# Making Strassen's weight sums in DRAM with accumulating transfers, during an earlier phase of the kernel

## The chip, the cores and the metric

The kernel runs on one core of one Trainium2 chip. The metric is the device time of one execution in microseconds (us). The kernel before was timed three times: 2057.39, 2060.06 and 2066.34 us, so its median is 2060.06 us. The profile is of one further execution.

## The reference

Two layers of a diffusion backbone run over 256 latent and 256 context tokens, model width 2048, all float32. Layer 0 is a bidirectional retention layer, layer 1 a windowed attention layer:

```python
for i in range(DEPTH):                      # DEPTH = 2
    mod_l = c_act @ ada_w[i] + ada_b[i]     # shift, scale, gate (latent); mod_c likewise for the context
    h_l = _rms_norm(x, norm_gain[i]) * (1 + sc_l) + sh_l          # h_c likewise
    if i % 2 == 0:
        y_l, y_c = _retention_mixer(h_l, h_c, ret_w_in, ..., ret_w_out, ...)
    else:
        y_l, y_c = _attention_mixer(...)
    x = x + gt_l * y_l
    if i < DEPTH - 1:
        ctx = ctx + gt_c * y_c

def finish(o, g):                           # the end of the retention layer
    on = o * rsqrt(mean(o * o) + EPS) * norm_gain
    return (on * silu(g)) @ w_out           # (512 x 4096) @ (4096 x 2048)
```

The change concerns the last line, the retention layer's output projection, and what runs before it.

## The kernel before, in words

**Precision.** TensorE multiplies in a rounded float32 format. Each operand is split into a high part (rounded, a cast on ACT) and a low part (source minus high, a subtraction on DVE), and products are summed from high x high, high x low and low x high. For a weight tile of 128 x 1024 elements, `split_w` does this: the cast `wh` (L131) and the subtraction `wl` (L112, which is the line of every such subtraction). A weight tile arrives by `load_raw` (L122) on SP's DMA queue into `wraw`; there are three buffers each of `wraw`, `wh` and `wl`.

**Phases, in order of time.** First the modulation of layer 0 and the first projections (to about 133 us); then the eight retention heads (to about 1222 us); then the output projection of the retention layer (to 1630 us); then the attention layer (to 2059 us).

**The heads.** Per head there are a gate, a query-key and a value projection, each of 8 weight pieces (`gemm_ws` or `gemm_ts`). After each piece a `hook` is called; the hooks are numbered by `state["n"]`, and a head has 24 (the first two and the last 16). A hook runs one entry of a list of small tasks: `output_tasks` of the head before (POOL adds up squares at L789 and takes the power `rs` at L239, TensorE then transposes `rs`), `score_tasks` with `decays` (POOL's power `dd`, L736). From the 33rd hook on it also runs two `ada_jobs`: a load `abraw` on SP (L672) and one or two products with running sums on DVE (L675). The program's planner fixes the order in which each engine issues its instructions, by priorities and by its own costs; `tc.issue_after(x)` ties an instruction behind x on x's engine.

**The output projection by Strassen.** The 4096 x 2048 weight is cut into 2 x 2 blocks and the operand likewise (the halves of the contraction, and latent against context tokens). Seven products, M1 to M7, replace eight. `parts` forms the operand sums of each head and puts them into DRAM (`uB_d`); `prep` (L649) loads them and splits them into high and low. Products were done in four stages: (M4, M1), (M5, M7), (M2, M6) and (M3). In `stage`, an output quarter r (0 to 3) takes four contraction quarters kq; for each r, kq and product, `weights` yields a split weight tile and `piece` does 8 high matmuls (L927, 512 columns) and 8 low ones (L924, 256 columns). Weights are loaded by `quarter` (L906, 512 KB each). Where a product needs the sum of two weight blocks, both are loaded and `comb` adds them on POOL (L911). Raw weight tiles go round a `ring` of seven buffers. `done` functions take the accumulators out (`merged` L932 to L937, `added` L941) into `x1`; `residual` (L960) applies the gate and adds the input, `square` (L950, L951) sums squares for the next norm; in the last stage `hook4` modulates the latent tokens for layer 1 (ACT at L1079, POOL through `comb`, then `modulate`).

Of the kernel before, what the change touches and what calls it, by code (L numbers as in the profile page):

```python
# [10 lines left out]
F32 = mybir.dt.float32  # L11
F32R = mybir.dt.float32r
# [9 lines left out]
T = 512  # L22
L = 256
# [28 lines left out]
def backbone(ctx: ExitStack, tc, xT_d, w0_d, wo0_d, w1_d, wo1_d, adaS_d, adaB_d,  # L52
# [39 lines left out]
    gam16 = const.tile([P, 8, 8], F32, name="gam16")  # L92
    lg2 = const.tile([P, 16], F32, name="lg2")

    ng = vec[:, V_NG:V_NG + 32].rearrange("p (l k) -> p l k", l=2)
# [15 lines left out]
    def sub(out, a, hi):  # L111
        return nc.vector.tensor_tensor(out=out, in0=a, in1=hi.bitcast(F32), op=ALU.subtract)  # L112
# [4 lines left out]

    last_lo, last_hi = [None], [None]

# [8 lines left out]
    def split_w(raw):  # L128
        wh = strm.tile([P, 2, 512], F32R, name="wh", tag="wh", bufs=3)
        wl = strm.tile([P, 2, 512], F32R, name="wl", tag="wl", bufs=3)  # L130
        last_hi[0] = nc.scalar.copy(wh, raw).ins  # L131
        last_lo[0] = sub(wl, raw, wh).ins
        return wh, wl

# [473 lines left out]
    def slot_l(s):  # L608
# [7 lines left out]
    R_, T_, h_, H_ = ([(n, i) for i in range(k)] for n, k in (("R", 10), ("T", 5), ("h", 8), ("H", 8)))  # L616
    home = {M4: R_[0:8], M1: R_[8:10] + T_[0:5] + H_[7:8], M5: h_, M7: H_[5:7] + R_[2:8],
            M2: R_[0:2] + R_[8:10] + T_[0:4], M6: T_[4:5] + H_[7:8] + R_[2:8], M3: h_}
    units = {}
# [34 lines left out]
    if True:  # L654
# [32 lines left out]

        jobs = ada_jobs()
        state = {"n": 0}

        def hook():
            state["n"] += 1
            if state["n"] > 32:
# [152 lines left out]
        for h in range(H):  # L846
# [20 lines left out]
            if h == 1:  # L867
                close_top()
        for _ in jobs:
            pass  # L870

# [25 lines left out]
    with tc.tile_pool(name="pc", bufs=1, side="right") as pc:  # L897
# [5 lines left out]

        def quarter(nh, kh, r, kq):
            t = raw_tile()
            nc.sync.dma_start(out=t.rearrange("p a t -> p (a t)"),  # L906
                              in_=wo0_d[nh, kh, r, kq].rearrange("p k c -> p (k c)"))
            return t

        def comb(out, a, b, op):  # L910
            nc.gpsimd.tensor_tensor(out=out, in0=a, in1=b, op=op)  # L911
            return out

# [24 lines left out]

        def added(out, acc):
            for c in (lat, cx):  # L940
                nc.vector.tensor_tensor(out=out, in0=acc[:, c], in1=out, op=ALU.add)  # L941

        def square(kb, c):
# [8 lines left out]

        def residual(kbs):

            xr = raw_tile()
            nc.sync.dma_start(out=xr, in_=xT_d[:, kbs[0]:kbs[-1] + 1, :])
            for i, kb in enumerate(kbs):
                for s in range(2):
                    c = (lat, cx)[s]
                    nc.vector.scalar_tensor_tensor(out=x1[:, kb, c], in0=x1[:, kb, c], scalar=gt0[:, kb, s:s + 1],  # L960
                                                   in1=xr[:, i, c], op0=ALU.mult, op1=ALU.add)
                nc.scalar.dma_start(out=x1_d[kb], in_=x1[:, kb, lat])
                square(kb, lat)

        def stage(ms, weights, done, hook):
            for r in range(4):
                accs = {m: [acc_tile() for _ in range(2)] for m in ms}
                n1, n2 = slice(2 * r, 2 * r + 2), slice(8 + 2 * r, 10 + 2 * r)
                for kq in range(4):
# [4 lines left out]
                    hook(r, kq)  # L974

        def weights1(r, kq):
            b, a = quarter(1, 1, r, kq), quarter(0, 0, r, kq)
            yield split_w(b)
            yield split_w(comb(a, a, b, ALU.add))

        def done1(r, m, accs, n1, n2):
            for j in range(2):
                merged(x1[:, 8 + 2 * r + j, lat if m == M4 else cx], accs[j], neg=(m == M4))
            if m == M1:
                comb(x1[:, n1, lat], x1[:, n2, cx], x1[:, n2, lat], ALU.add)

        def hook1(r, kq):
            if kq == 1:
                prep(M5, [2 * r, 2 * r + 1])
            if (r, kq) == (2, 2):  # L990
                prep(M7, [0, 1])
            if r == 3 and kq > 1:
                prep(M7, [2 * kq - 2, 2 * kq - 1])
# [6 lines left out]
        def done2(r, m, accs, n1, n2):  # L1000
            if m == M5:
                for j in range(2):
                    merged(x1[:, 2 * r + j, cx], accs[j])
            else:
                for j in range(2):
                    added(x1[:, 2 * r + j, lat], accs[j])
                comb(x1[:, n1, lat], x1[:, n1, lat], x1[:, n1, cx], ALU.subtract)

        def hook2(r, kq):
            if r and kq == 2:  # L1010
                residual([2 * r - 2, 2 * r - 1])
            if kq == 1:
                prep(M2, [2 * r, 2 * r + 1])
            if (r, kq) == (2, 2):
                prep(M6, [0, 1])
            if (r, kq) == (0, 0):
                prep(M7, [6, 7])
            if r == 3 and kq > 1:
                prep(M6, [2 * kq - 2, 2 * kq - 1])

        def weights3(r, kq):
            a, b, c = quarter(1, 0, r, kq), quarter(1, 1, r, kq), quarter(0, 0, r, kq)
            yield split_w(comb(b, a, b, ALU.add))
            yield split_w(comb(c, a, c, ALU.subtract))

        def done3(r, m, accs, n1, n2):
            if m == M2:
                t = tmp[:, r % 2]
                for j in range(2):
                    merged(t[:, j], accs[j])  # L1030
                comb(x1[:, n2, lat], x1[:, n2, lat], t, ALU.add)
                nc.vector.tensor_tensor(out=x1[:, n2, cx], in0=x1[:, n2, cx], in1=t, op=ALU.subtract)
            else:
                for j in range(2):
                    added(x1[:, 8 + 2 * r + j, cx], accs[j])

        def hook3(r, kq):
            if (r, kq) == (0, 0):
                prep(M6, [6, 7])
            if kq == 2:  # L1040
                residual([2 * r + 6, 2 * r + 7])
            if kq == 1:
                prep(M3, [2 * r, 2 * r + 1])
# [9 lines left out]

        def weights4(r, kq):
            yield split_w(quarter(0, 0, r, kq))

        def done4(r, m, accs, n1, n2):
            t = tmp4[:, r % 2]
            for j in range(2):
                merged(t[:, j], accs[j])  # L1060
                for kb in (2 * r + j, 8 + 2 * r + j):
                    nc.vector.scalar_tensor_tensor(out=x1[:, kb, cx], in0=t[:, j], scalar=gt0[:, kb, 1:2],
                                                   in1=x1[:, kb, cx], op0=ALU.mult, op1=ALU.add)
                    square(kb, cx)

# [3 lines left out]

        def hook4(r, kq):  # L1070

            if r == 0:
                return
            n = 4 * (r - 1) + kq
            for kb in range(16 * n // 12, 16 * (n + 1) // 12):
                if kb % 2 == 0:
                    hl[kb // 2] = r1.tile([P, 2, T], F32R, name="hl", tag=f"hl{kb // 2}")
                with tc.issue_after(last_hi[0]), tc.issue_after(last_lo[0]):
                    nc.scalar.activation(x1[:, kb, lat], x1[:, kb, lat], AF.Copy, scale=gs1[:, kb, 0:1])  # L1079
                    comb(x1[:, kb, lat], x1[:, kb, lat], rB[:, lat], ALU.mult)  # L1080
                    modulate1(kb, 0)

        stage((M3,), weights4, done4, hook4)
        bp = token_rstd(pc, [ssq, rB], (2, 4))

# [307 lines left out]
```

## Time and profile before

| What | Before |
|---|---|
| time, median of 3 runs | 2060.06 us |
| the profiled execution: time, and span of its trace | 2060.75 us, 2059.0 us |
| TensorE busy, mean granted clock | 1969.8 us (96%), 0.987 |
| DVE, ACT, POOL busy | 1447.7, 764.6, 603.0 us |
| moved by DMA | 385.83 MB, mean 187 GB/s |
| HBM read and written | 365.71 MB and 18.38 MB |
| weight loads of the output projection | 176 of 512 KB |

"PE" is TensorE's matmuls and "PEld" its weight loads, which overlap; a busy PE is not a PE at its peak. A group of instructions is shown as line, engine, operation, out<-in by the program's names, shapes, count, then busy time in us and mean time in ns, then the engine's idle time before them and what ended it. A wait "A <- B: 31.1, 32, 3.2" says that A's engine sat idle for 31.1 us in 32 gaps, the longest 3.2 us, until B ended. The granted clock is TensorE's share of full speed. The DMA share is the mean busy share of the core's 16 DMA engines.

### The profile page before, as it was taken

How to read it: one execution, taken by the hardware profiler on the slowest of the kernel's cores; microseconds unless marked ns; L12 is line 12 of the kernel's file. 1: busy time of each engine (PE TensorE's matmuls, PEld its weight loads, DVE VectorE, ACT ScalarE, POOL GpSimd, SP SyncE). 2: the span in 40 equal slices, each digit the busy share in tenths (PEclk: the TensorE clock that was granted, in tenths of full speed). 3: DMA queues.
4: the chain of work that ended last, by engine and by line, in shares of the span. 5: the costliest groups of instructions: out<-in, count | busy, mean ns of one | idle time of the engine just before them, and what ended most of it. 6: DMA issues, size and time to landing. Idle time of an engine off the chain costs nothing. (4 is left out here: it accounts for less than half of the span.)

```text
span 2059.0 us, 26306 instructions
## 1 busy us (share of the span) xinstructions
PE 1969.8 (96%) x9589; PEld 1622.3 (79%) x9589; DVE 1447.7 (70%) x2481; ACT 764.6 (37%) x1147; POOL 603.0 (29%) x235
## 2 busy tenths in 40 slices
PE   6999999999999999999999999977778999999999
PEld 3678888888888888888888888766657888888888
DVE  5575225887887887885556457899888864777765
ACT  3243223232232232332322334433324733666653
POOL 0226424205106115033002035687775210000001
PEclk9999999999999999999999999999889999999999
DMA  9953235655755765665554456677666334444455
GB/s 377 411 199 95 94 123 174 210 184 159 224 181 162 226 177 180 209 187 184 194 182 138 128 180 221 223 246 263 223 231 234 101 108 134 151 133 145 143 186 172
DMA packets 141506, 385.83 MB, mean 187 GB/s; under 512 B 14464, under 2 KB 33216, under 8 KB 137664
## 3 DMA queue, kind: packets, MB, share of 16 engines
q1 hardware_dynamic: 122512, 363.66, 53.5%
q10 hardware_dynamic: 18864, 20.49, 3.0%
q8 instruction: 75, 1.23, 0.2%
q14 instruction: 55, 0.45, 0.1%
HBM read 365.71 MB, written 18.38 MB: 187 GB/s over the span
## 5 line engine op out<-in xcount | busy, mean ns | idle before, releaser
L112 DVE TENSOR_TENSOR wl<-wraw,wh 128x1024 fp32r<-128x1024 f32 x416 | 596.6, 1439 | 372.6 <-ACT wh L131 368.5
L131 ACT CAST wh<-wraw 128x1024 fp32r<-128x1024 f32 x415 | 433.6, 1050 | 893.7 <-PE acc L139 311.5
L138 PE MATMUL acc<-hT_h,wh 128*128 128x512 f32 x928 | 363.6, 392 | 0.9 <-DVE r_l L112 0.9
L140 PE MATMUL acc<-hT_h,wl 128*128 128x512 f32 x928 | 362.0, 390 | 0.0
L139 PE MATMUL acc<-hl,wh 128*128 128x512 f32 x928 | 361.8, 390 | 0.0
L675 DVE SCALAR_TENSOR_TENSOR ajunk<-abraw,crow 128x512 bf16<-128x512 f32 x448 | 341.8, 763 | 9.2
L736 POOL TENSOR_TENSOR dd<-two,dd 128x128 f32<-128x128 f32 x8 | 168.0, 21003 | 446.6 <-DVE dd L734 446.6
L140 PE MATMUL acc<-wh,hl 128*128 128x512 f32 x704 | 275.0, 391 | 0.0
L911 POOL TENSOR_TENSOR wraw<-wraw 128x1024 f32<-128x1024 f32 x80 | 237.0, 2984 | 91.2 <-DMA wraw<-in_wo 75.3
L138 PE MATMUL acc<-wh,hT_h 128*128 128x512 f32 x576 | 224.4, 390 | 0.0
L139 PE MATMUL acc<-wl,hT_h 128*128 128x512 f32 x576 | 224.4, 390 | 0.0
L138 PEld LDWEIGHTS acc<-hT_h,wh 128*128 128x128 f32 x928 | 174.7, 188 | 37.8 <-DVE r_l L112 1.3
L140 PEld LDWEIGHTS acc<-hT_h,wl 128*128 128x128 f32 x928 | 174.7, 188 | 36.7
L139 PEld LDWEIGHTS acc<-hl,wh 128*128 128x128 f32 x928 | 174.7, 188 | 35.0
L140 PEld LDWEIGHTS acc<-wh,hl 128*128 128x128 f32 x704 | 132.6, 188 | 27.6
L239 POOL TENSOR_TENSOR rs<-ms,mhalf 128x4 f32<-128x4 f32 (+1 forms) x23 | 32.7, 1422 | 322.0 <-DVE ms L233 304.1
L138 PEld LDWEIGHTS acc<-wh,hT_h 128*128 128x128 f32 x576 | 108.2, 188 | 22.3 <-issue 0.2
L139 PEld LDWEIGHTS acc<-wl,hT_h 128*128 128x128 f32 x576 | 108.2, 188 | 21.8
L789 POOL TENSOR_TENSOR ossq<-ossq,osq 128x512 f32<-128x512 f32 x24 | 33.9, 1412 | 263.5 <-ACT osq L783 263.5
L803 POOL TENSOR_TENSOR ue<-sg 128x512 f32<-128x512 f32 x38 | 66.5, 1766 | 73.8 <-DVE sg L793 46.3
L927 PE MATMUL acc<-bop,wh 128*128 128x512 f32 x224 | 65.8, 432 | 19.1 <-ACT wh L131 11.9
L138 PE MATMUL acc<-wh,hl 128*128 128x512 f32 x192 | 75.9, 395 | 0.0
(263 smaller groups left out, 2936.8 us busy)
## 6 DMA issues: line engine op xcount, KB each, us to landing
wraw<-in_w SPq DMA_DIRECT2D x272, 512.0 KB, 3.5
wraw<-in_wo SPq DMA_DIRECT2D x176, 512.0 KB, 4.3
abraw<-in_adaB SPq DMA_DIRECT2D x256, 256.0 KB, 3.3
araw<-in_adaS SPq DMA_DIRECT2D x28, 1024.0 KB, 13.0
wraw<-uB_d SPq DMA_DIRECT2D x20, 512.0 KB, 4.1
uB_d<-ue ACTq DMA_DIRECT2D x38, 256.0 KB, 3.2
araw<-in_adaS SPq DMA_DIRECT2D x8, 512.0 KB, 9.4
uB_d<-sg ACTq DMA_DIRECT2D x16, 256.0 KB, 2.5
```

The lines of the kernel that those rows point to most:

```text
L112: return nc.vector.tensor_tensor(out=out, in0=a, in1=hi.bitcast(F32), op=ALU.subtract)
L131: last_hi[0] = nc.scalar.copy(wh, raw).ins
L138: nc.tensor.matmul(ps, lhsT=ah, rhs=bh, start=start, stop=False, skip_group_check=skip)
L139: nc.tensor.matmul(ps, lhsT=ah, rhs=bl, start=False, stop=False, skip_group_check=skip)
L140: return nc.tensor.matmul(ps, lhsT=al, rhs=bh, start=False, stop=stop, skip_group_check=skip).ins
L239: nc.gpsimd.tensor_tensor(out=rs, in0=ms, in1=mhalf.to_broadcast([P, n]), op=ALU.pow)
L675: nc.vector.scalar_tensor_tensor(out=junk, in0=raw, scalar=1.0, in1=crow[:, t, q * 512:(q + 1) * 512], op0=ALU.mult, op1=ALU.mult, accum_o ...
L736: nc.gpsimd.tensor_tensor(out=dd, in0=two.to_broadcast([P, P]), in1=dd, op=ALU.pow)
L789: nc.gpsimd.tensor_tensor(out=ssq, in0=ssq, in1=sq, op=ALU.add)
L803: (nc.vector if now else nc.gpsimd).tensor_tensor(out=ue, in0=x, in1=y, op=op)
L911: nc.gpsimd.tensor_tensor(out=out, in0=a, in1=b, op=op)
L927: nc.tensor.matmul(accs[j], lhsT=wk, rhs=b, start=(kq == 0 and k == 0), stop=False)
```

## The change

The weight blocks that products M2, M6, M5 and M7 need as sums are no longer loaded in pairs and added by POOL during the projection. They are formed in DRAM (`wS_d`, 4 sums of 8 MiB) during the heads: for each half quarter row (1 MiB) a plain DRAM-to-DRAM copy of the first block on ACT's DMA queue, and one step of the generator later an accumulating DRAM-to-DRAM transfer of the second block, issued by POOL behind a one-column copy (`pin`) that reads the newest `wl`. There are 32 such pairs. The hook runs a step at hooks 12, 14, 16, 28, 30 and 32, then at the offsets 8, 10, 12, 14 and 22 of each following 24 up to the 160th, and after the 162nd.

The products then go in the order (M4, M1) together, and M5, M7, M2, M3, M6 one by one, each with one load a piece. In the first stage M1's weight sum is made by negating the loaded block on ACT and accumulating the other block onto it by a transfer that POOL issues, so signs change downstream (`ngt`, `neg=True`). `comb` moves from POOL to DVE; the latent modulation of layer 1 is spread over M3's second half and M6, wholly on ACT and DVE; `residual` takes latent and context tokens apart.

```diff
+    wS_d = dram.tile([4, 4, 4, P, 4, 256], F32, name="wS_d")
+    SUMS = (((1, 0), (1, 1)), ((1, 0), (0, 0)), ((0, 0), (0, 1)), ((0, 1), (1, 1)))
+    def sum_jobs():
+        todo = [(i, r, slice(2 * q, 2 * q + 2)) for i in (2, 3, 0, 1) for r in range(4) for q in range(2)]
+        for n in range(len(todo) + 1):
+            if n < len(todo):
+                i, r, q = todo[n]
+                with tc.issue_after(last_hi[0]):
+                    nc.scalar.dma_start(out=wS_d[i, r, q], in_=wo0_d[(*SUMS[i][0], r, q)])
+            if n:
+                i, r, q = todo[n - 1]
+                pin = nc.gpsimd.tensor_copy(pin_t, last_wl[0][:, 0, 0:1].bitcast(F32)).ins
+                with tc.issue_after(pin):
+                    nc.gpsimd.dma_start(out=wS_d[i, r, q], in_=wo0_d[(*SUMS[i][1], r, q)], accum_op=ALU.add,
+                                        max_dma_last_dim=4096)
+            yield
...
+            if n in (12, 14, 16, 28, 30, 32) or 32 < n < 161 and (n - 33) % 24 in (8, 10, 12, 14, 22) or n > 162:
+                next(sums, None)
...
         def comb(out, a, b, op):
-            nc.gpsimd.tensor_tensor(out=out, in0=a, in1=b, op=op)
-            return out
+            return nc.vector.tensor_tensor(out=out, in0=a, in1=b, op=op)
...
+        def single(m, src, done, hook):
+            def weights(r, kq):
+                yield split_w(quarter(src, r, kq))
+            stage((m,), weights, lambda r, m, *a: done(r, *a), hook)
...
         def weights1(r, kq):
-            b, a = quarter(1, 1, r, kq), quarter(0, 0, r, kq)
+            b, a = quarter(wo0_d[1, 1], r, kq), raw_tile()
             yield split_w(b)
-            yield split_w(comb(a, a, b, ALU.add))
+            nc.scalar.activation(a, b, AF.Copy, scale=-1.0)
+            nc.gpsimd.dma_start(out=a.rearrange("p a t -> p (a t)"),
+                                in_=wo0_d[0, 0, r, kq].rearrange("p k c -> p (k c)"), accum_op=ALU.add)
+            yield split_w(a)
...
-        def weights2(r, kq):
-            a, b, c = quarter(0, 0, r, kq), quarter(0, 1, r, kq), quarter(1, 1, r, kq)
-            yield split_w(comb(a, a, b, ALU.add))
-            yield split_w(comb(c, b, c, ALU.subtract))
...
+        def done_m7(r, accs, n1, n2):
+            for j in range(2):
+                for c in (lat, cx):
+                    z = x1[:, 2 * r + j, lat]
+                    comb(z, z, accs[j][:, c], ALU.subtract)
...
         stage((M4, M1), weights1, done1, hook1)
-        stage((M5, M7), weights2, done2, hook2)
-        stage((M2, M6), weights3, done3, hook3)
-        residual([14, 15])
+        single(M5, wS_d[2], done_m5, hook_m5)
+        single(M7, wS_d[3], done_m7, hook_m7)
+        single(M2, wS_d[0], done_m2, hook_m2)
+        residual(two(7), 0)
...
+        def done_m6(r, accs, n1, n2):
+            for j in range(2):
+                kb = 8 + 2 * r + j
+                for c in (lat, cx):
+                    nc.vector.scalar_tensor_tensor(out=x1[:, kb, cx], in0=accs[j][:, c], scalar=gt0[:, kb, 1:2],
                                                    in1=x1[:, kb, cx], op0=ALU.mult, op1=ALU.add)
-                    square(kb, cx)
+                square(kb, cx)
...
+        def latents(kb):
...
+            with tc.issue_after(last_hi[0]), tc.issue_after(last_lo[0]):
+                scaled(x1[:, kb, :], x1[:, kb, :], kb, gs1, rB, (0,))
+                modulate1(kb, 0)
+        def hook_m3(r, kq):
+            if r and kq == 2:
+                residual(two(r - 1), 1)
+            if r and kq == 3:
+                residual(two(r + 3), 1)
+            if r >= 2 and kq % 2:
+                latents(2 * (r - 2) + kq // 2)
+        def hook_m6(r, kq):
+            if r == 0 and kq < 2:
+                residual(two(3 + 4 * kq), 1)
+            n = 4 * r + kq
+            for kb in range(4 + 12 * n // 16, 4 + 12 * (n + 1) // 16):
+                latents(kb)
...
+        single(M3, wo0_d[0, 0], done_m3, hook_m3)
+        single(M6, wS_d[1], done_m6, hook_m6)
```

More of the change, by code (lines that the diff above doesn't have):

```diff
@@ L132, in split_w @@
         last_lo[0] = sub(wl, raw, wh).ins
+        last_wl[0] = wl
         return wh, wl
@@ L686, in ada_jobs @@
             open_top("wx")
-        jobs = ada_jobs()
+        jobs, sums = ada_jobs(), sum_jobs()
         state = {"n": 0}
@@ L868, in backbone @@
                 close_top()
-        for _ in jobs:
-            pass
+        for g_ in (jobs, sums):
+            for _ in g_:
+                pass
         sg = pb.tile([P, 4, 512], F32, name="sg", tag="sg")
@@ L1026, in done3 @@
[L1026 to L1039, printed above, removed]
+                prep(M5, two(r))
@@ new lines, in hook_m7, with done_m2, hook_m2 @@
+        def hook_m7(r, kq):
+            if kq == 1:
+                prep(M3, two(r))
+            if r and kq == 2:
+                residual(two(r - 1), 0)
+        def done_m2(r, accs, n1, n2):
+            t = tmp[:, r % 2]
+            for j in range(2):
+                merged(t[:, j], accs[j])
+            comb(x1[:, n2, lat], x1[:, n2, lat], t, ALU.add)
+            comb(x1[:, n2, cx], x1[:, n2, cx], t, ALU.subtract)
+        def hook_m2(r, kq):
+            if kq == 1:
+                prep(M6, two(r))
@@ L1083, in backbone @@
-        stage((M3,), weights4, done4, hook4)
+        def latents(kb):
+            if kb % 2 == 0:
+                hl[kb // 2] = r1.tile([P, 2, T], F32R, name="hl", tag=f"hl{kb // 2}")
+            with tc.issue_after(last_hi[0]), tc.issue_after(last_lo[0]):
[8 more added lines that the diff above has]
+                latents(2 * (r - 2) + kq // 2)
```

95 lines of the change are left out of this document (33 added, 62 removed).

## The prediction

> **What bounds the kernel now.** I read the page's first part, then the busy time by stage, then TensorE's waits in the stage that stands out, then what the engines in front of it were doing there.
>
> ```profile
> span 2059.0 us, 26306 instructions
> PE 1969.8 (96%) x9589; PEld 1622.3 (79%) x9589; DVE 1447.7 (70%) x2481; ACT 764.6 (37%) x1147; POOL 603.0 (29%) x235
> ```
>
> Busy time in stretches (length; busy time of PE, PEld, DVE, ACT, POOL; granted clock; DMA share; GB/s). The first table goes by phases (the heads with the modulation sums are 339 to 1109, the output projection 1222 to 1630), the second takes the projection's own four stages:
>
> ```profile
> 133.00:339.00 206.00, 206.00 (x938) 171.52 (x938) 86.45 (x154) 67.88 (x100) 87.74 (x13) 1.00 0.36 118
> 339.00:1109.00 770.00, 769.08 (x3522) 640.96 (x3521) 596.97 (x1309) 209.23 (x292) 182.83 (x58) 1.00 0.60 189
> 1222.00:1630.00 408.00, 346.17 (x1802) 286.23 (x1801) 355.56 (x315) 172.22 (x252) 274.52 (x109) 0.95 0.66 222
> 1746.00:2059.00 313.00, 308.11 (x1665) 263.53 (x1664) 220.89 (x362) 183.55 (x301) 18.20 (x20) 1.00 0.49 155
> ...
> 1221.80:1315.90 94.10, 90.76 (x513) 78.48 (x512) 76.46 (x63) 46.73 (x64) 54.60 (x21) 1.00 0.64 216
> 1315.90:1444.50 128.60, 102.08 (x519) 82.01 (x518) 117.40 (x88) 46.52 (x63) 106.09 (x37) 0.96 0.72 246
> 1444.50:1581.70 137.20, 107.10 (x508) 85.91 (x509) 118.93 (x95) 43.09 (x58) 96.93 (x35) 0.88 0.66 223
> 1581.70:1630.20 48.50, 46.63 (x269) 40.20 (x267) 43.16 (x73) 36.10 (x69) 16.90 (x17) 1.00 0.49 166
> ```
>
> The heads keep TensorE full at clock 1.00: nothing can be won there, only lost. The projection does not. Its floor comes from one piece of a product (8 high and 8 low matmuls), from start to start in a stretch without waits:
>
> ```profile
> 1598.00 2.00 PE L927 MATMUL acc<-hT_h,wh 128*128 128x512 f32 x8
> 1599.84 1.11 PE L924 MATMUL acc<-hT_h,wl 128*128 128x256 f32 x8
> 1600.79 2.00 PE L927 MATMUL acc<-hT_h,wh 128*128 128x512 f32 x8
> ```
>
> A piece is 2.79 us; a product has 16, so 44.6 us; seven products need 312.5 us. The projection takes 408.4, so 95.9 us are lost: 94.1 - 89.3 = 4.8 in stage 1 (M4, M1), 39.3 in stage 2 (M5, M7), 47.9 in stage 3 (M2, M6), 3.9 in stage 4 (M3 alone). What TensorE waits for there (us in total, times, longest), and the operations ahead of it (first DVE in the heads, then DVE in stages 2 and 3, then POOL and ACT in the whole run; count, busy us, mean ns):
>
> ```profile
> PE acc L924 <- DVE wl L112: 31.1, 32, 3.2
> PE acc L927 <- ACT wh L131: 19.4, 13, 3.1
> PE acc L927 <- DVE x L937: 6.4, 7, 1.2
> ...
> L112 DVE TENSOR_TENSOR wl<-wraw,wh 128x1024 fp32r<-128x1024 f32 x163 | 201.3, 1236 | 180.8 <-ACT wh L131 180.8
> L112 DVE TENSOR_TENSOR wl<-wraw,wh 128x1024 fp32r<-128x1024 f32 x32 | 75.6, 2373 | 7.5 <-ACT wh L131 7.4
> L112 DVE TENSOR_TENSOR wl<-wraw,wh 128x1024 fp32r<-128x1024 f32 x34 | 71.3, 2106 | 9.2 <-ACT wh L131 9.0
> L911 POOL TENSOR_TENSOR wraw<-wraw 128x1024 f32<-128x1024 f32 x80 | 237.0, 2984 | 91.2 <-DMA wraw<-in_wo 75.3
> L131 ACT CAST wh<-wraw 128x1024 fp32r<-128x1024 f32 x415 | 433.6, 1050 | 893.7 <-PE acc L139 311.5
> ```
>
> The same subtraction takes 1.24 us in the heads and 2.1 to 2.4 us in stages 2 and 3, where POOL is busy 0.71 to 0.82 of the time, nearly all of it with weight sums. DVE is then busy 117 of 129 us, and TensorE waits for wl and for wh, whose casts stand behind POOL's sums. On top, the clock granted after the gaps is 0.96 and 0.88: 0.04 x 128.6 + 0.12 x 137.2 = 21.6 us of the 95.9.
>
> **The change, part by part.** *Weight sums leave POOL.* All 80 additions (237 us of POOL) go. Each later product then needs one load, one cast, one subtraction per piece. The row nearest to such a stage is stage 4: one product, one load a piece, POOL busy 16.90 of 48.5 us: it lost 3.9 us with DVE busy 43.16. I price the other stages by DVE's work, from these rows (POOL quiet, or PSUM as source):
>
> ```profile
> L112 DVE TENSOR_TENSOR hT_h<-wraw,hT_h 128x512 fp32r<-128x512 f32 x6 | 3.9, 682 | 2.4 <-ACT hT_h L115 2.4
> L937 DVE TENSOR_TENSOR x<-acc,x 128x256 f32<-128x256 f32 x6 | 2.5, 415 | 0.0
> L960 DVE SCALAR_TENSOR_TENSOR x<-x,gt,wraw 128x256 f32<-128x256 f32 x4 | 1.8, 477 | 0.0
> L951 DVE TENSOR_TENSOR ssq<-ssq,pm 128x256 f32<-128x256 f32 x12 | 4.9, 411 | 0.0
> L1032 DVE TENSOR_TENSOR x<-x,tmp 128x512 f32<-128x512 f32 x1 | 0.7, 681 | 0.0
> ```
>
> Every stage has 16 subtractions, 19.8 us. M5 adds 16 operand splits (10.9), 8 merges (3.3), 4 sums moved from POOL (2.7): 36.7 us. M7: 8 splits, 16 subtractions from PSUM, 6 residuals with squares (0.48 + 0.41): 37.1. M2: 8 splits, 8 merges, 8 wide sums, 10 residuals: 42.9. M3: 8 merges, 8 wide sums, 12 context residuals (6 with a square), 4 latent modulations of two operations: 40.6. M6: 16 scaled adds from PSUM, 8 squares, 4 residuals, 12 latent modulations (11.5, of which half was POOL's): 45.0, level with TensorE's 44.6. At stage 4's ratio (43.16 of 48.5, 0.89) I take 47 us for M5 and M7, 48.5 for M2 and M3, 45.0/0.89 = 50.6 for M6: 241.6 in all. With 2 of 5 accumulators in use instead of 4, the 6.4 us behind L937 go too; with gaps this short the clock stays as in stage 4.
>
> *Stage 1.* ACT gains 16 negations (1.05 us each, as its casts of that size), 16.8 us on 46.7 of 94; POOL's queue issues 16 accumulating loads. The second weight of a piece arrives by load, negation, issue, accumulate. No row shows an accumulate into SBUF. Below: the plain load, 4.3 us to landing (row next), which replaces a POOL sum of 3 us, so up to 4.8 us are won. Above: if ACT's queue holds the next negation behind the cast that waits for this landing, a pair of pieces takes cast, negation, landing of about 6, cast, 9.2 us for 5.6, 58 us lost. The planner runs ahead over 7 raw tiles, as POOL's sums did, so I stay near the low end: 97 us, 3 more than now.
>
> *Sums in the heads.* 32 copies (ACT's queue) and 32 accumulates (POOL's), 1 MiB each, and 32 one-column copies on POOL that wait for the newest wl. Five jobs fall in each head's 24 hooks, four of them two hooks apart; 770 us for 128 hooks is 6.0 us a hook. The DMA rows that bound them:
>
> ```profile
> 0.00:100.00 100.00, 81.15 (x473) 50.73 (x474) 52.14 (x122) 34.54 (x53) 15.90 (x11) 1.00 1.01 396
> GB/s 377 411 199 95 94 123 174 210 184 159 224 181 162 226 177 180 209 187 184 194 182 138 128 180 221 223 246 263 223 231 234 101 108 134 151 133 145 143 186 172
> araw<-in_adaS SPq DMA_DIRECT2D x28, 1024.0 KB, 13.0
> wraw<-in_wo SPq DMA_DIRECT2D x176, 512.0 KB, 4.3
> ...
> SPq L122 <- DVE wl L112: 840.1, 248, 13.7
> ACT wh L131 <- PE acc L139: 311.5, 79, 5.3
> ```
>
> Flat out the engines move 396 GB/s: a 1 MiB copy costs 2.65 us of them. An accumulate has no row. Its price A lies between a copy (2.65) and 13.0 us, what 1 MiB took to land with the queues full. [...] In two hooks (12.0 us) the present loads need 0.60 x 12.0 = 7.2 us; with copy and accumulate 15.2: four pairs leave 12.6 us of backlog. The cover: SP spends 840 us waiting for a free raw tile and ACT 311 us for TensorE to free wh, so loads run some 20 us ahead (three raw and two spare split pieces, less what is in flight). 12.6 fits, and the 16 hooks up to the next burst absorb it; if the cover were gone, each of five bursts would cost its backlog, 63 us. I charge 6 us for the heads, bounds 0 and 63. POOL's queue: behind a late accumulate stand the ossq sums, rs and dd; TensorE's transposes wait for rs. The jobs sit at hooks 8 to 14 and 22, after output_tasks and before decays, and each waits for a copy issued two hooks earlier: charged nothing, covered by those 12 us.
>
> [...]
>
> *The sum.* 97 + 241.6 = 338.6 for the projection against 408.4: 69.8 won; 6 given back. The profiled execution took 2060.75 us (span 2059.0), 0.7 over the median 2060.06: 2060.75 - 63.8 = 1997.
>
> **The rivals.**
> *Accumulates dear (slower).* Place: the four-job bursts of five heads. With price A the stall is 5 x (4 x (A - 2.15) - 20). It cancels the 69.8 us at A = 10.6. At 13.0 it is 117 us: 1991 + 117 = 2108. For it: DMA share 0.60 already, no row of an accumulate, three queues sharing the engines. Against: the stock above, and A must be four times a copy.
> *Memory rate, half the gain.* If writes and double reads count against the 396 GB/s, two hooks of a burst hold 189 x 12.0 = 2.3 MB of loads, 2.1 MB of copy and 3.1 MB of accumulate: 7.5 MB, 19.0 us of 12.0. That is 28 us of backlog in four pairs, 8 over the cover, five times: 40 us, 1991 + 40 = 2031. For it: a burst demand of 626 GB/s, which no slice shows. Against: those 396 GB/s are loads into SBUF, whose writes did not touch the memory. [...]
> *Stage 1 in series.* The 58 us above: 1997 + 55 = 2052, near no change. Against: POOL's sums ran ahead in the same ring.
> *DVE takes the bound.* If the singles pace at 55 us a product (DVE at 0.82 of the time), 275 instead of 241.6: 2030. For it: M6 has 45.0 us of DVE work; against: stage 4's row.
>
> **How the numbers follow.** Forecast 0.58, own range 1972 to 2015 (projection between 320 and 350, heads 0 to 10). Memory rate 0.14, DVE 0.05, stage 1 in series 0.08, dear accumulates 0.15. About 0.5% (10 us) is what a measurement here can tell from none. Faster: 0.58 + 0.14 + 0.05 and a quarter of the series case, 0.79. Same: half the series case and a little of the dear one, 0.06. Slower: the rest, 0.15. The range 1972 to 2070 leaves out most of the dear case and a sliver below.
>
> **What the profile after would show.** Right: no 128x1024 additions on POOL, wl near 1.24 to 1.35 us from stage 2 on, the projection about 339 us at clock 0.99 or more, TensorE still full between 339 and 1109 with the DMA share at 0.85 to 0.95. Wrong: TensorE waiting for wl or wh in the heads after the loads landed late (dear accumulates or memory), ACT's casts waiting for the accumulating load in stage 1, or DVE full while TensorE idles in M6.

## The result, and the profile after

The changed kernel took 2044.47 us (median of 6 runs, 2039.21 to 2052.4), the kernel before 2059.5 beside it (6 runs, 2057.39 to 2066.34): a ratio of 0.9926, with a 95% interval of 0.990 to 0.995. It is faster by 15 us; 63 were forecast. The profiled execution took 2052.4 us, at the upper end of its runs; the sums below are made against that one.

The page's first lines, its DMA queues and its DMA issues (KB each, median us to landing):

```profile
span 2050.6 us, 26254 instructions
PE 1970.6 (96%) x9589; PEld 1626.8 (79%) x9589; DVE 1323.2 (65%) x2502; ACT 771.4 (38%) x1147; POOL 387.3 (19%) x207
...
q1 hardware_dynamic: 118800, 338.49, 48.5%
q0 software_dynamic: 11008, 41.95, 10.9%
...
wraw<-in_w SPq DMA_DIRECT2D x272, 512.0 KB, 4.2
abraw<-in_adaB SPq DMA_DIRECT2D x256, 256.0 KB, 4.7
wS_d<-in_wo POOLq DMA_DIRECT2D x32, 1024.0 KB, 12.6
```

Then the stretches: the heads, and the projection's stage 1 and its five single products (length; busy time of PE, PEld, DVE, ACT, POOL; clock; DMA share; GB/s).

```profile
339.00:1109.00 770.00, 735.20 (x3264) 602.98 (x3263) 560.80 (x1252) 201.76 (x281) 205.68 (x102) 0.98 0.81 248
1280.40:1399.70 119.30, 102.65 (x526) 87.55 (x525) 61.87 (x75) 56.70 (x75) 18.44 (x17) 0.90 0.69 175
1399.70:1626.00 226.30, 225.83 (x1295) 198.08 (x1294) 183.00 (x278) 124.62 (x181) 0.72 (x1) 1.00 0.72 239
```

The projection begins at 1280.4 us where it began at 1221.8: the heads lose 58.6 us. It ends at 1626.0 and so takes 345.6 us where it took 408.4: 62.8 won. What follows it is 4.2 us shorter. Together 8.4 us, as the two profiled executions differ (2060.75 and 2052.4).

So the gain is there, and the heads hand it back. In the 770 us from 339 to 1109 there ran 3264 matmuls in place of 3522; at the old pace the 258 missing ones are 56 us. TensorE idled 34 of them. Most of the rest is clock: 0.98 granted on average over 770 us is an estimated 15 us, and after some of the waits the matmuls come at half their rate (0.43 us apart in place of 0.23, below). What it waited for (339 to 1280; us in total, times, longest):

```profile
PE acc L142 <- DVE wl L113: 21.4, 12, 3.9
PE acc L140 <- ACT wh L132: 7.9, 4, 3.9
```

And VectorE, from 339 to 1109:

```profile
DVE ajunk L696 <- DMA abraw<-in_adaB: 118.8, 36, 7.9
```

One such wait in order of time, first on VectorE:

```profile
596.89 0.69 DVE L696 SCALAR_TENSOR_TENSOR ajunk<-abraw,crow 128x512 bf16<-128x512 f32 x1 [7.70 <-DMA abraw<-in_adaB]
```

Then on TensorE:

```profile
594.63 0.39 PE L141 MATMUL acc<-hl,wh 128*128 128x512 f32 x1
598.78 0.80 PE L142 MATMUL acc<-hT_h,wl 128*128 128x512 f32 x1 [3.76 <-DVE wl L113]
599.37 0.63 PE L140 MATMUL acc<-hT_h,wh 128*128 128x512 f32 x1
...
603.64 0.63 PE L141 MATMUL acc<-hl,wh 128*128 128x512 f32 x1
604.38 0.39 PE L140 MATMUL acc<-hT_h,wh 128*128 128x512 f32 x1
```

VectorE stands 7.70 us on a late tile of the modulation sums (abraw); the subtraction wl behind it in its order comes late, and TensorE waits 3.76 us. The weight was not late. Its cast was ready at 590.04, on ScalarE:

```profile
588.99 1.05 ACT L132 CAST wh<-wraw 128x1024 fp32r<-128x1024 f32 x1 [1.06 <-DMA wraw<-in_w]
```

The same holds for all eight waits for a wl of over 0.9 us, 21 us in all: the cast lay ready 5 to 11 us before VectorE, held up by an abraw product, began the subtraction. After the wait shown, TensorE's matmuls start 0.43 us apart instead of 0.23 until 604: a wait of 3.76 us, and 5 us at half rate behind it. A shorter wait was enough, too: after one of 1.88 us the matmuls start 0.43 us apart from 812.54 to 815.9.

```profile
811.92 0.50 PE L141 MATMUL acc<-wl,hT_h 128*128 128x512 f32 x1 [1.88 <-DVE wl L113]
```

### The profile page after: what moved, and what is told of

Read it like the earlier page. It is cut to its first block, busy times and chain, and to the rows that moved or that the text cites. A ratio compares the mean times of both kernels' runs of the same rounds, so it can differ in the third digit from the quotient of the medians.

```text
span 2050.6 us, 26254 instructions
## 1 busy us (share of the span) xinstructions
PE 1970.6 (96%) x9589; PEld 1626.8 (79%) x9589; DVE 1323.2 (65%) x2502; ACT 771.4 (38%) x1147; POOL 387.3 (19%) x207
## 3 DMA queue, kind: packets, MB, share of 16 engines
q0 software_dynamic: 11008, 41.95, 10.9%
HBM read 416.04 MB, written 85.49 MB: 245 GB/s over the span
## 5 line engine op out<-in xcount | busy, mean ns | idle before, releaser
L113 DVE TENSOR_TENSOR wl<-wraw,wh 128x1024 fp32r<-128x1024 f32 x416 | 510.7, 1232 | 365.5 <-ACT wh L132 355.5
L142 PE MATMUL acc<-hT_h,wl 128*128 128x512 f32 x928 | 368.2, 397 | 22.0 <-DVE wl L113 22.0
L140 PE MATMUL acc<-hT_h,wh 128*128 128x512 f32 x928 | 367.8, 396 | 6.5 <-ACT wh L132 6.5
L142 PE MATMUL acc<-wh,hl 128*128 128x512 f32 x704 | 275.9, 392 | 0.0
L142 PEld LDWEIGHTS acc<-hT_h,wl 128*128 128x128 f32 x928 | 177.2, 191 | 65.2 <-DVE wl L113 27.8
L142 PEld LDWEIGHTS acc<-wh,hl 128*128 128x128 f32 x704 | 132.9, 189 | 27.8
L321 POOL COPY pin_t<-wl 128x1 f32<-128x1 f32 x32 | 16.4, 513 | 472.2 <-DVE wl L113 472.2
L955 PE MATMUL acc<-r_h,wh 128*128 128x512 f32 x240 | 69.4, 420 | 15.2 <-ACT wh L132 10.8
L141 PE MATMUL acc<-wl,hl 128*128 128x512 f32 x192 | 74.8, 389 | 0.0
## 6 DMA issues: line engine op xcount, KB each, us to landing
wS_d<-in_wo POOLq DMA_DIRECT2D x32, 1024.0 KB, 12.6
```

The costliest lines, as they stand in the source:

```text
L140: nc.tensor.matmul(ps, lhsT=ah, rhs=bh, start=start, stop=False, skip_group_check=skip)
L141: nc.tensor.matmul(ps, lhsT=ah, rhs=bl, start=False, stop=False, skip_group_check=skip)
L142: return nc.tensor.matmul(ps, lhsT=al, rhs=bh, start=False, stop=stop, skip_group_check=skip).ins
L955: nc.tensor.matmul(accs[j], lhsT=wk, rhs=b, start=(kq == 0 and k == 0), stop=False)
```

## Experiments

Base in all: the kernel before, 2058 to 2061 us in each batch. "Start" is the projection's first matmul (before 1221.8, after 1280.4).

**Which transfer costs it.** Three kernels without parts of the pairs.

```
no_sums:       - the copy and the accumulate of every pair; M5, M7, M2, M6 load one block of wo
copies_only:   - the accumulate of every pair
plain_second:  - accum_op=ALU.add   (the second transfer overwrites; same queue, packets, places)
```

> Left out: all 64 DRAM-to-DRAM transfers in the heads; M5, M7, M2 and M6 load a single weight block in place of the sum, same sizes. POOL's one-column copies that wait for wl stay. Theory A (the transfers take the DMA engines from the loads in the heads): the projection starts near 1222 us again instead of 1280, TensorE is full from 339 to 1109, and the time falls by some 55 us, to about 1990. Rival B (the waits that the change puts on POOL and ACT, or the new planned order, hold the heads up): the projection still starts after 1260 and the time stays above 2025.

> Left out: the 32 accumulating transfers; the 32 plain copies and POOL's waits stay, so the stored sums lack one block. By engine time, with 2.65 us per MiB copy, two hooks of a burst hold 7.2 + 2.7 = 9.9 us of 12.0: no backlog. Theory A with the accumulates as the cost: the projection starts at 1222 to 1232, time 1990 to 2000. Rival C (copies inside DRAM hurt by themselves, their long rows hold the engines): a start past 1245 and a time above 2010.

> The second transfer is a plain copy issued by POOL with the same split instead of an accumulate (the stored sums lack the first block). It tells the double read from the queue and the bytes. If the accumulate's price is its second read (about 5.6 us of the 16 engines per MiB against 2.7), demand in a burst falls from 15.2 to 12.6 us of 12.0 and most of the heads' loss goes: start of the projection at 1225 to 1240, time 1990 to 2008. Rival D (POOL's queue and its descriptors are what slows the loads): a start past 1260, time above 2025.

Measured: no_sums 1992.04 us (ratio 0.967, 0.9648 to 0.9693), start 1220.8. copies_only 1995.0 (0.9693, 0.9666 to 0.972), start 1227.7. plain_second 1996.09 (0.9696, 0.9674 to 0.9718), start 1230.9. The stretch from 339 to 1109 in no_sums:

```profile
339.00:1109.00 770.00, 769.01 (x3522) 640.98 (x3521) 597.75 (x1309) 209.84 (x293) 194.06 (x83) 1.00 0.61 189
```

and in plain_second:

```profile
339.00:1109.00 770.00, 764.99 (x3492) 635.08 (x3493) 585.90 (x1305) 214.34 (x298) 203.69 (x106) 1.00 0.75 258
```

The transfers are the cause; the 32 pins on GpSimd and the hooks, which no_sums keeps, cost nothing. By the starts the copies cost 7 us, a plain second transfer 3 more. That the second one adds costs the other 49.5. plain_second moves 258 GB/s, more than the changed kernel's 248, and its heads lose a sixth as much: the bytes that the profile counts are not it. It counts as many bytes read with the accumulates as without, though (416.04 MB from the memory in both kernels), so whether an accumulate reads its destination as well, and whether the price lies in such a read or in the addition, stays open. The price itself shows in the packets of the second transfers, here plain_second's from 150 to 1190:

```profile
q0 software_dynamic: 8704, 33.56, 8.4%
```

8.4% of 1040 us over 32 MiB is 2.7 us of the 16 engines for 1 MiB, half of what an accumulate takes (5.6, below).

**Spacing.** The hooks of each 24 at which a pair is issued, evenly in place of bunched.

```
-(n - 33) % 24 in (8, 10, 12, 14, 22)
+(n - 33) % 24 in (2, 7, 12, 17, 22)
```

> Same transfers, but at offsets 2, 7, 12, 17 and 22 of each 24 hooks instead of 8, 10, 12, 14 and 22. Theory A in its burst form (engine time runs out only while four pairs come close together; the mean demand is 0.6 + 0.29): backlogs of one pair are covered, the heads lose 5 to 20 us instead of 58, time 1995 to 2012. Rival E (each long transfer delays the loads it meets, whenever it comes): the 25 pairs still cost 1.5 us or more each, 40 us and more together, time 2025 to 2050.

Measured: 2046.09 us (10 runs; 0.9942, 0.9923 to 0.9962), start 1283.7: no gain. That looked like the end of the burst as the cause, but it was not, as best_places shows below. The loads were in time again, and TensorE's waits for wl at L142 fell from 21.4 us to 1.0. Queue q1 (all of SP's loads) in the 60 us from 400, in the changed kernel (packets, MB, share of the engines' time):

```profile
q1 hardware_dynamic: 3720, 9.27, 43.0%
```

in no_sums:

```profile
q1 hardware_dynamic: 4663, 11.36, 61.3%
```

and in spread:

```profile
q1 hardware_dynamic: 4744, 11.51, 55.5%
```

A different wait took the place of the old one, once a head. TensorE, GpSimd and ScalarE of spread around one of them:

```profile
567.28 0.79 PE L140 MATMUL acc<-hT_h,wh 128*128 128x512 f32 x1 [5.35 <-ACT sg L744]
551.95 0.94 POOL L323 DMA_DIRECT2D wS_d<-in_wo  x1
564.21 1.94 POOL L828 TENSOR_TENSOR ue<-sg 128x512 f32<-128x512 f32 x1 [11.32 <-DMA uB_d<-ue]
566.18 0.33 ACTq L832 DMA_DIRECT2D uB_d<-ue  x1
566.63 2.06 ACT L744 ACTIVATE sg<-acc 128x512 f32<-128x512 f32 x4 [9.41 <-DMA wraw<-in_w]
```

The accumulate of place 2 starts at 551.95, where a head's operand sums are stored. GpSimd's next ue needs the buffer that a store uB_d is reading, and waits 11.32 us for it; ScalarE has that ue's store in its order, so the gate's Silu behind it starts at 566.63 and TensorE waits 5.35 us. (The label of ACT's own wait names a load; the issue at 566.18, right after the ue that began at 564.21, is what it stood on.)

**Does VectorE's order matter.**

```
-in0=raw, scalar=1.0, in1=crow[...]
+in0=crow[...], scalar=1.0, in1=crow[...]
```

> Leaves out: the adaLN products multiply crow with itself instead of with the loaded tile abraw, so their values are wrong; every load of abraw is still made, at its place in SP's queue, but VectorE never waits for one. Theory A1 (VectorE stands in order behind the slowed abraw loads, 118.8 us of waits in the changed kernel, and the wl splits behind it come late): most of the PE's 25 us of waits for wl go, and with them some of the clock's 17 us after them; projection starts at 1235 to 1255 in place of 1280.5, time 2000 to 2020. Rival A2 (the weights' own loads, wraw, land too late as well, so the ACT casts and not the products set the pace): start stays at 1270 or later, 2030 to 2045.

Measured: 2285.3 us (1.1094). It doesn't answer the question. With no reader the loads were not throttled, and SP issued 69 and then 128 of them in a row ahead of the weights:

```profile
240.83 97.73 SPq L693 DMA_DIRECT2D abraw<-in_adaB  x69
...
428.88 194.43 SPq L693 DMA_DIRECT2D abraw<-in_adaB  x128
```

One thing is to be had from it. From 800 to 1000 us no abraw load was left to make, eight accumulates were issued beside the weights' loads alone, and TensorE was busy 200.00 of 200 us at clock 1.00. In this stretch, beside the weights' loads alone, the accumulates cost nothing. (In the first head, where no abraw loads run either, 11 of them do cost something: see best_places.)

**Stage 1 alone.**

```
-b, a = quarter(wo0_d[1, 1], r, kq), raw_tile()
+b, a = quarter(wo0_d[1, 1], r, kq), quarter(wo0_d[0, 0], r, kq)
-nc.scalar.activation(a, b, AF.Copy, scale=-1.0)
-nc.gpsimd.dma_start(out=a..., in_=wo0_d[0, 0, r, kq]..., accum_op=ALU.add)
+nc.gpsimd.tensor_tensor(out=a, in0=a, in1=b, op=ALU.subtract)
```

> Stage 1 of the projection alone is changed back: a and b are both plainly loaded and GpSimd subtracts them in SBUF, with no negation on ScalarE and no accumulating transfer. Theory C (the ring's tiles are held longer by the negation, its queueing on ScalarE and the 7.5 us landing of the accumulate): stage 1 falls from 119.3 to about 95 us, time 2018 to 2026, the heads unchanged (start 1276 to 1285). Rival D (stage 1 waits for its raw loads or its start behind the heads whatever forms the sums): 115 us or more, 2040 to 2046.

Measured: 2037.65 us (0.9897, 0.9875 to 0.992), start 1278.9, stage 1 104.5 us in place of 119.3, between the two theories. By the medians the whole is 7 us faster than the changed kernel, and the intervals overlap. In the changed kernel TensorE, ScalarE's negations and GpSimd's issues had waited there (1280 to 1400):

```profile
PE acc L955 <- ACT wh L132: 10.8, 4, 4.6
```

```profile
ACT wraw L1014 <- DMA wraw<-in_wo: 20.8, 4, 6.4
```

```profile
POOL wraw L1015 <- ACT x L960: 45.4, 5, 12.3
POOL wraw L1015 <- ACT wraw L1014: 27.8, 7, 8.9
```

That chain is gone from s1_pool; of the 10 us left to the 94.1 of before, 6.2 are one wait for the merge x (L961), and the clock granted in this stage was 0.93, where it was 1.00 before. In half_sums below the same code took 92.1, so this wait is not of stage 1's form; why it is there in one and not the other stays open.

Without stage 1's accumulates queue q0 holds the heads' 32 alone:

```profile
q0 software_dynamic: 8704, 33.56, 8.8%
```

8.8% of 2035.6 us over 32 MiB is 5.6 us of the 16 engines for 1 MiB.

**Smaller packets.** `max_dma_last_dim=4096` of the heads' accumulates to 2048.

> Only the accumulating transfers' packets in the heads are halved, from 4 KB to 2 KB. Theory E (each DMA engine takes the queues' packets in turn, and an accumulate packet of 0.34 us stands before each load packet of 0.1 to 0.15 us, so loads slow down by the packet): loads beside an accumulate land sooner, the heads lose 25 to 45 us in place of 59, time 2010 to 2032. Rival F (what counts is the engines' time per byte): no change, 2038 to 2050. Rival G (most of a packet's 0.34 us is a fixed cost): 32 MB then cost nearly twice the 5.5 us a MiB, and the time is above 2060.

Measured: 2056.57 us (0.9985, 0.9973 to 0.9998), start 1291.2; the accumulates land after 15.5 us in place of 12.6. Less the 44 us of stage 1 (10.9% of 2050.6 in the changed kernel against s1_pool's 179), 11.6% of 2053.1 us leaves 194 us, 6.1 a MiB. None of the three theories: hardly dearer, and the heads end 11 us later than in the changed kernel, with each accumulate in the way for longer. The loads gained next to nothing by it in the first burst as a whole, 2.61 MB for 2.50 in the same 24 us (401 to 425):

```profile
q0 software_dynamic: 826, 1.66, 38.1%
q1 hardware_dynamic: 1006, 2.61, 31.9%
```

**Moving the places, first try.** s1_pool with hooks 5, 8, ... 32 in the first head, then 6, 11, 15, 21 of each 24.

> Stage 1 by GpSimd as in the run above, and the 32 pairs of transfers set elsewhere: every third hook from 5 to 32 in the first head (18 us apart), then at places 6, 11, 15 and 21 of each 24, away from the start of a head where ScalarE issues the stores uB_d between its own work and GpSimd makes ossq and rs. In the evenly spread run the accumulate at place 2 made such a store land after some 10 us, GpSimd's next ue waited 11.3 us for it, ScalarE's queue 9.4 us for that, and the PE 5.35 us for the gate's Silu. If the loss comes from who happens to wait during an accumulate, the heads lose 25 to 40 us in place of 59 and stage 1 gives back 22: 1995 to 2012. If any accumulate costs the heads its 1.8 us whatever stands beside it, the heads lose 55 to 60 again: 2018 to 2026.

Measured: 2092.0 us (1.0159, 1.0136 to 1.0182), start 1334.2. Worse than before, by another wait again. GpSimd in one head:

```profile
524.22 21.14 POOL L761 TENSOR_TENSOR dd<-two,dd 128x128 f32<-128x128 f32 x1 [34.51 <-DVE dd L759]
545.35 3.94 POOL L814 TENSOR_TENSOR ossq<-ossq,osq 128x512 f32<-128x512 f32 x3
```

The decays' power, 21 us, waited for VectorE's part of it (L759) until 524.22, when ossq's input came too; in the changed kernel it is done 1.8 us before that input comes. So TensorE's sums of ossq (L249) waited up to 9.4 us in four heads (34.4 in all); its waits for ScalarE's Silu came to another 18.9. Why VectorE's part comes so late isn't shown.

**Second try: only the place that the trace had named.** s1_pool with spread's places less place 2, and the first head, where no abraw loads run, taking 11 pairs.

```
-n in (12, 14, 16, 28, 30, 32) or 32 < n < 161 and (n - 33) % 24 in (8, 10, 12, 14, 22)
+n in range(6, 27, 2)          or 32 < n < 161 and (n - 33) % 24 in (7, 12, 17, 22)
```

> Stage 1 by GpSimd as in s1_pool (2037.65 us, projection from 1278.9), and of the pairs' places only those changed: 11 pairs in the first head at every second hook from 6 to 26, where no abraw loads run, then places 7, 12, 17 and 22 of each 24, which are the evenly spread ones without place 2. Theory H (the loss of the spread run came from the one accumulate a head that slows the stores uB_d, 3.7 to 5.4 us of waiting for the gate's Silu and then half clock for 6.8 us): start at 1235 to 1258, time 1994 to 2018. Rival I (whatever place they have, 32 accumulates take the loads' share of the DMA engines and the heads pay for it): start at 1270 or later, 2028 to 2042.

Measured: 2000.81 us (0.9711, 0.9693 to 0.973), start 1243.1, as theory H has it: 37 us less than s1_pool, 57 less than the kernel before. The heads:

```profile
200.00:339.00 139.00, 131.91 (x589) 107.62 (x589) 38.89 (x52) 34.96 (x41) 36.75 (x29) 0.99 0.85 248
339.00:1109.00 770.00, 765.15 (x3490) 635.13 (x3489) 588.77 (x1296) 208.84 (x294) 211.39 (x93) 1.00 0.78 241
```

From 339 to 1109 only 32 matmuls (7 us) are missing, with 20 accumulates there; the changed kernel lost 56 us with 26. The first head, with more pairs, loses 51 matmuls (11 us) from 200 to 339, where the kernel before ran 640. There is no burst any more. One accumulate a head still starts among the uB_d stores, but GpSimd's ue behind it waits 4.17 us and not 11.32, and TensorE waits for no Silu:

```profile
545.99 0.94 POOL L323 DMA_DIRECT2D wS_d<-in_wo  x1
551.10 1.82 POOL L828 TENSOR_TENSOR ue<-sg 128x512 f32<-128x512 f32 x1 [4.17 <-DMA uB_d<-ue]
```

**Half the bytes.** s1_pool at the changed kernel's places, each pair 512 KB (every second piece); GpSimd adds the other pieces in the projection. Then the same with best_places' places.

> s1_pool with half of the sums' bytes: the 32 pairs stay at the places of the changed kernel but move 512 KB each (every second piece), and GpSimd adds the other pieces in the projection from two loads. Theory J (threshold: in a burst the load queue falls behind, 9.27 MB in place of 11.4 in 60 us, some 11 us, and the stock covers about half of that): with half the bytes the lag of about 6 us is covered, start at 1225 to 1245. The five products go from 226.3 to 230 to 245 us, since GpSimd needs 2.98 us for a sum in every 5.58 us and the ring has three raw tiles where it had two. Time 1988 to 2016. Rival K (loss in proportion to the bytes): start at 1248 to 1255, time 2010 to 2030.

> half_sums with the places of best_places. If theories H and J both hold, nothing is left of the heads' loss but its copies: start at 1222 to 1235, time 1980 to 2005. If the places alone mattered it equals best_places within 8 us plus what GpSimd's sums cost the products.

Measured: 2020.4 (0.9807, 0.9784 to 0.9831) and 2013.45 us (0.9776, 0.9751 to 0.9801). The heads do as J says: starts 1226.6 and 1221.5, a loss of 5 us and of none. Half the bytes in the same burst cost under a tenth. But the singles pay for it, 274.0 and 267.2 us in place of 226.3:

```profile
1318.70:1592.70 274.00, 242.84 (x1296) 206.01 (x1296) 225.31 (x278) 122.44 (x183) 84.38 (x32) 0.95 0.75 256
```

DVE is slowed beside GpSimd's sums, as it was in the projection before (225.31 us for the 278 instructions that took 183.00). My 230 to 245 was too low.

**Half the modulation's loads.** The changed kernel, loading half of each abraw tile.

> The changed kernel with its own places and stage 1; only the abraw loads are halved: 256 of each tile's 512 columns are loaded, and VectorE's product, as long as before, reads these 256 twice. So half of in_adaB is left out of the sum. Theory J (the load queue lags in a burst: it moved 9.27 MB in 60 us where 11.4 were wanted): wraw and abraw are about equal in bytes, so some 8.5 MB are wanted, less than the 9.27 that the queue got beside the accumulates; no lag, PE's waits for wl are gone, projection from 1222 to 1240 in place of 1280.5, time 1986 to 2006. Rival L (an accumulate holds something else, VectorE's or GpSimd's way into SBUF or the weights' own landing, and the bytes of the loads don't matter): start at 1265 to 1282, time 2030 to 2048.

Measured: 2029.42 us (0.9854, 0.9818 to 0.9889), start 1259.9: between the theories, a third of the heads' loss recovered. The loads from 401 to 425, the first 24 us of the burst, in no_sums:

```profile
q1 hardware_dynamic: 2133, 5.16, 69.4%
```

in the changed kernel:

```profile
q0 software_dynamic: 537, 2.09, 43.8%
q1 hardware_dynamic: 978, 2.50, 30.3%
```

and in half_ada:

```profile
q1 hardware_dynamic: 1174, 2.25, 26.7%
```

A fifth more packets and fewer bytes, since half of them are smaller: some 3.9 MB were wanted (three quarters of 5.16), 2.25 came. So beside these pairs a load pays more by its packets than by its bytes, and the lag is 24 x (1 - 2.25/3.9) = 10 us where the changed kernel's is 12.4. Where one accumulate was alone with the loads, in the changed kernel (417 to 423):

```profile
q0 software_dynamic: 232, 0.91, 77.0%
q1 hardware_dynamic: 233, 0.63, 29.3%
```

and in packets_2k, in the same 6 us:

```profile
q0 software_dynamic: 352, 0.69, 62.9%
q1 hardware_dynamic: 355, 1.00, 46.4%
```

That is one load packet for one accumulate packet in both. An accumulate's packet of 4 KB takes 0.770 x 6 x 16 / 232 = 0.32 us, one of 2 KB 0.17, a load's 0.12 or 0.13. So at both packet sizes the loads beside the one accumulate got as many packets as it had, and with 2 KB packets their share was 46% in place of 29%. Why packets_2k's heads gain nothing by that stays open: each of its accumulates has twice the packets and lands 2.9 us later, and in the 24 us with the copies the loads got 31.9% for 30.3%. That the loads fall behind is shown; that the load packets themselves slow down is not: 0.43 x 60 x 16 / 3720 = 0.11 us each in the burst from 400 to 460, in no_sums 0.613 x 960 / 4663 = 0.13.

**The copies' packets** cut to 4 KB, in the changed kernel and in best_places. (The expectation below puts them at 32 KB, which is the mean over a copy's 32 records; 16 of these hold its whole MiB, 64 KB each, as in packets_2k from 405 to 407: 16 records, 1.05 MB.) And best_places with hooks 3, 6, ... 27 in the first head.

> The changed kernel; only the copies' packets are cut from 32 KB to 4 KB. In half_ada 18 abraw loads of half the size landed after 7.7 us in place of 9.0, as many in the same 60 us, so a load pays by the packet beside the pair. Theory M (the DMA engines take packets in turn, and a copy's packet of 32 KB, some 1.3 us, holds up the loads' packets behind it): loads in a burst land sooner, the burst's 9.27 MB rise above 10, start 1255 to 1270, time 2018 to 2034. Rival N (the accumulates alone hold the loads): no change, 2039 to 2050. Rival O (more packets on ScalarE's queue take more turns from the loads, not fewer): start later than 1285, above 2050.

> best_places (2000.81 us, start 1243.1) with the copies' packets of 4 KB. By M the 13 us lost in the first head and the 9 us from 339 to 1109 shrink: 1988 to 1997. By N 1997 to 2004. By O 2003 to 2015.

> best_places with the first head's pairs at every third hook from 3 to 27 (9 of them, 18 us apart) in place of 11 at every second, and the others at the end. If two pairs of hooks a pair is too close for the first head (its PE waits 9.1 us from 130 to 339, 279.0 to 282.4 at half clock), the start comes 5 to 12 us earlier and the time is 1989 to 1998; if what is pushed to the end costs as much there, 1998 to 2010.

Measured: copy_4k 2044.6 us (0.9933, 0.9909 to 0.9958), start 1282.4, no change, as rival N has it: the size of the copies' packets is not what holds up the loads. best_copy_4k 1997.69 (0.9697, 0.9679 to 0.9715): not told apart from best_places, whose interval it overlaps. best_first_head 2006.61 (0.974, 0.972 to 0.9761), start 1252.8: no gain from pairs further apart. TensorE now waited 6.9 us at once for a wh before 339 us, and the clock from 270 to 339 was 0.90, where 11 closer pairs had cost waits of under 2. This head lost 13 matmuls more than best_places (3 us), the stretch to 1109 another 11 (2 us), and the rest of the 9.7 us lies behind, where pairs were pushed to.

## Why the prediction was right or wrong

- **That the projection is the place:** right. All 80 additions are gone, and the clock is 1.00 in the singles. Its price, 338.6 us forecast and 345.6 measured, came this close partly by luck: the singles took 15.3 us less than forecast and stage 1 22.3 more.
- **The singles:** better than forecast, 226.3 us for 241.6. The step at fault is stage 4's ratio (0.89 of the time DVE-busy) applied as if VectorE set the pace. DVE was busy 183.00 of 226.3, TensorE 225.83.
- **Stage 1:** 119.3 for 97. The rival's chain (ACT's queue holds the next negation, the landing takes 7.5 us) was real, but worth about 15 us (119.3 against s1_pool's 104.5), not 58; the other 10 of the 25 lost stay when it is gone. I stayed at its low end because GpSimd's sums had run ahead in the same ring; a negation on ScalarE stands in the same queue as the casts, GpSimd's sums do not.
- **The heads, 6 us for 58.6: the step that failed.** The price in it was right: A was put at 5.3 us a MiB and measured 5.6, and at that price the formula of the dear-accumulates rival gives no stall at all. That an accumulate fetches twice the bytes, from which the 5.3 came, no run shows: 416.04 MB were read in the changed kernel as in plain_second, while the engines' time for 1 MiB was 5.6 us against 2.7. Three other terms were wrong.
  - *The rate of the backlog.* I shared the engines by the bytes asked for. Beside one accumulate they went by packets (233 of the loads for 232 of its own), and the loads got less: 2.50 MB of 5.16 in the first 24 us, a lag of 24 x (1 - 2.50/5.16) = 12.4 us, as much as I allowed for all four pairs. Part of it is that the first two pairs came closer than two hooks, their accumulates at 404.6 and 412.9.
  - *The cover.* In this burst TensorE first waited at 425.5 us, so the lag it absorbed was about 12 us, not 20. I read 20 us of lead from SP's and ACT's waits over the weights' tiles. VectorE's order holds the products on abraw too, with four tiles and two used at each hook, and a wl behind such a product did not pass it in any of the eight waits. That this order and not late weights made TensorE wait for wl is seen in the trace, where the casts lay ready 5 to 11 us earlier; the run made to test it, no_read, did not tell.
  - *What a wait costs.* I priced stalls at their length. With the half clock after them 34 us idle became 56.
- **Memory rate:** its time came close (2031), by luck as far as the runs show; its mechanism was not seen. Load packets were no slower in a burst (0.11 us each, in no_sums 0.13). plain_second moved 311 GB/s from 400 to 460, and with the 7.25 MB of its transfers inside the memory counted as read and written, 432, above the 396 that the rival took as the limit; it lost no matmul, where the changed kernel lost 32 at 304. The 304 hold no second read of an accumulate; no run shows whether there is one, so a cost of it at the memory is not ruled out. plain_second:

```profile
400.00:460.00 60.00, 60.00 (x266) 49.69 (x266) 46.11 (x109) 19.80 (x31) 3.06 (x6) 1.00 0.85 311
```

The changed kernel:

```profile
400.00:460.00 60.00, 55.23 (x234) 44.56 (x234) 37.48 (x85) 15.17 (x21) 6.30 (x9) 0.97 0.99 304
```

- **GpSimd's queue, charged nothing:** right here (0.6 us of waits for rs), but by the places, not by a rule: in both_mended it cost 34.4 us.
- **The cover's place in the range:** the bounds of 0 and 63 us for the heads held the 58.6. The weight was wrong: nothing but the 20 us of lead spoke for 6, and no row showed that lead in the burst's stretch.

## What to carry to other kernels

A background transfer is not free because the engines have time for its bytes (here the DMA share was 0.60 before and 0.81 with them, and the heads lost 58.6 us): ask what share its queue takes while it is in flight, and whether the tightest consumer beside it has that much lead. Count the lead at the tile with the smallest stock that stands in the same engine's order, and price a stall of TensorE with the slow clock after it (here 34 us idle became 56). Before giving up on work placed in the background, read which wait ended last at each place: moving the same 32 pairs was worth 37 us one way and cost 54 the other.

## What the runs showed of the hardware

An accumulating transfer inside the memory took 5.6 us of the 16 engines for 1 MiB and 12.6 us to land; the same transfer without the addition took 2.7 us and landed after 8.9. Halving its packets raised that to about 6.1 us and 15.5. Beside one alone the loads got one packet for each of its packets: 233 for 232 at 4 KB, 29% of the engines' time, and 355 for 352 at 2 KB, 46%. A wait of 3.76 us was followed by some 5 us of matmuls at half rate, one of 1.88 us by 3.4 us.
